# A depthwise convolution of 31 taps shared out anew between TensorE, VectorE and GpSimd

## The chip, the cores and the metric

The program runs on one core of one Trainium2 chip. A core has five engines that work side by side, each through its own queue in order: TensorE (PE; PEld is its weight load), VectorE (DVE), ScalarE (ACT), GpSimd (POOL) and SyncE (SP, which here only issues DMAs). The metric is the device time of one execution in microseconds; lower is better.

## The reference, cut to what matters

Two transformer blocks on 256 tokens with 1024 features: the first is SwiGLU, mixed attention, SwiGLU; the second is a convolution module, a feed-forward layer, an attention layer and another feed-forward layer. The change lies in the convolution module:

```python
def conformer_conv(hn, w_pw1, b_pw1, w_dw, b_dw, ln_g, ln_b, w_pw2, b_pw2):
    u = hn @ w_pw1 + b_pw1
    a, g = jnp.split(u, 2, axis=-1)
    u = a * jax.nn.sigmoid(g)
    u = lax.conv_general_dilated(u, w_dw[:, None, :], ...,       # depthwise: each channel by itself,
            padding=((30, 0),), feature_group_count=D_MODEL) + b_dw   # 31 taps back in time
    u = layernorm(u, ln_g, ln_b)
    u = jax.nn.silu(u)
    return u @ w_pw2 + b_pw2
```

## The kernel before

**Tiles.** Activations lie feature-major: 128 features on the partitions, 256 tokens along the free axis, so 1024 features are 8 tiles of 128x256.

**Weights.** All large weights come through one stream of chunks of 128x1024 (`in_wts`): SP loads a chunk into `raw` (5 buffers), ACT copies it to a rounded upper part `hi` (L231), and DVE subtracts to get the lower part `lo` (L235); `hi` and `lo` have 4 buffers each. A chunk holds 8 blocks of 128x128, and each block is used by three matmuls of 256 columns (L252 to L254: upper weights by upper activations, upper by lower, lower by upper), so 24 matmuls per chunk. In the stage "conv" a split is one instruction of 1024 columns; in other late stages it is two of 512.

**The convolution stage** (`conv`, L1126 to L1230) loops over 8 tiles. `pw1(n)` makes the two halves of tile n with 2 x 8 blocks (two chunks, so 16 chunks for the stage), DVE scales both out of PSUM (L1153, L1156), ACT applies tanh and bias, DVE joins them into `cu`, 30 columns of zeros and then 256 tokens (L1160). The zeros are GpSimd memsets (L1159). ACT also copies the tile into `cx`, with even and odd tokens on two halves of the partitions (L1166); its 32 columns of zeros are GpSimd memsets too (L1163), and `cx` has two buffers.

`conv_out(n)` shares the 31 taps. With `LAGS = 11`, TensorE does the last 21 taps as 11 matmuls in plain float32 for each half of the tile (L1181), with the taps on diagonals of 128x128 matrices `cw`, loaded by SP (9 of 16), or `dw`, built on DVE during the SwiGLU before (7 of 16, `tap_matrices`). ACT puts the result back in place as `cb` (L1184). `REST = TAPS + 1 - 2 * LAGS` = 10 taps are left to DVE: two chains of multiply-adds over shifted views of `cu` (L1193 for the first of each chain, L1195 for the others), whose sums are added (L1196), and from tile 1 on shifted by the first tile's mean (L1198). `stats(n)` adds the two results (L1203) and adds to the sum and the sum of squares of the layer norm (L1217 and L368).

**What sets the order.** A scheduler with a timeline of its own lays out each engine's queue at build time; on the chip each engine then follows its queue in order, waiting on semaphores. The layer norm's sums (L376 on PE, bank `pt`) need all eight tiles; behind them the order is written by hand.

Of the kernel before, what the change touches and what calls it, by code (L numbers as in the profile page):

```python
# [9 lines left out]
F32 = mybir.dt.float32  # L10
# [3 lines left out]
ALU = mybir.AluOpType  # L14
AX = mybir.AxisListType

P = 128
T = 256
D = 1024
KD = D // P  # L20
# [7 lines left out]
TAPS = 31  # L28
LAGS = 11
# [87 lines left out]
class Kern:  # L117
# [28 lines left out]
    def phase(self, name):  # L146
        """A pool for the tiles of one phase; closed when the next one opens."""
        if self.ph is not None:
            self.ph.close()
        if name == "ffn0":  # L150
            self.taps.close()
        self.ph = ExitStack()
        self.cycle = CYCLE.get(name, CYCLE["ffn"])
        self.stage = name
        self.name = name
        self.pp = self.ph.enter_context(self.tc.tile_pool(name=name, bufs=2, reuse_waits="pool"))
        if name == "f2w2":
            self.taps = ExitStack()
            self.tp = self.taps.enter_context(self.tc.tile_pool(name="taps", bufs=1, side="right"))
# [25 lines left out]
    # weights  # L185
# [17 lines left out]
    def raw_chunk(self):  # L203
        """A chunk of weights as they are; raw_weight() says which."""
        self.loaded += 1
        raw = self.rawp.tile([P, CH * P], F32, tag="raw", name=self.nm("raw"))
        self.nc.sync.dma_start(raw, self.ap["wts"][self.loaded])
        return self.loaded, raw
# [5 lines left out]
    def prefetch(self, two=False):  # L214
        """Load and split one more chunk of the weights; or leave the lower parts to a second step."""
        nc = self.nc
        self.loaded += 1
        chunk = self.loaded
        raw = self.rawp.tile([P, CH * P], F32, tag="raw", name=self.nm("raw"))
        pieces = 2 if chunk == 0 else 1  # L220
        step = CH * P // pieces
        for i in range(pieces):
            s = slice(i * step, (i + 1) * step)
            nc.sync.dma_start(raw[:, s], self.ap["wts"][chunk, :, s])
        hi = self.hip.tile([P, CH * P], F32R, tag="hi", name=self.nm("hi"))
        lo = self.lop.tile([P, CH * P], F32R, tag="lo", name=self.nm("lo"))
        piece = PIECE.get(self.stage, 4)
        h = piece * P
        def high(i):
            s = slice(i * h, (i + 1) * h)  # L230
            nc.scalar.activation(hi[:, s], raw[:, s], AF.Copy)  # L231

        def low(i):
            s = slice(i * h, (i + 1) * h)
            nc.vector.tensor_tensor(lo[:, s], raw[:, s], hi[:, s].bitcast(F32), op=ALU.subtract)  # L235

        self.ready.append((chunk, hi, lo))
        n = CH // piece
        if two:
            for i in range(n):  # L240
                high(i)
            return lambda: [low(i) for i in range(n)]
        for i in range(n):
            high(i)
            low(i)

    def mm3(self, out, pairs, first=True, last=True):
        """out += sum over (stationary (hi, lo), moving (hi, lo)) pairs."""
        nc = self.nc
        n = len(pairs)  # L250
        for i, ((sh, sl), (mh, ml)) in enumerate(pairs):
            nc.tensor.matmul(out, sh, mh, start=(first and i == 0), stop=False)  # L252
            nc.tensor.matmul(out, sh, ml, start=False, stop=False)  # L253
            nc.tensor.matmul(out, sl, mh, start=False, stop=(last and i == n - 1))  # L254

    def dense(self, name, c0, X, width=P):
        """A feature-major output tile [width, T] in a bank."""
        b = self.bank()
        out = b[:width, :T]
        self.mm3(out, [(self.weight(name, k, c0, width), X[k]) for k in range(len(X))])  # L260
        return out

    def dense_steps(self, name, c0, X, done):
        """As dense(), in steps; done() takes the output."""
# [7 lines left out]
    def early_steps(self, name, n, X, outs):  # L272
        """The output tile n of a dense, from inputs that are still to come."""
# [7 lines left out]
    def fill(self, n):  # L281
        """n steps of the dense work in line."""
# [9 lines left out]
    def finish(self, key):  # L292
        """All steps in line up to those of a key."""
# [12 lines left out]
    def pipeline(self, units, start, second, lag, w, keep):  # L306
        """The units' stages, one unit behind the other, and the work in line between them,
        of which some is kept for the last units."""
# [24 lines left out]
    # splits  # L333
# [21 lines left out]
    # norms  # L355

    def square_into(self, acc, x, last=False):
        """x * x added to the sums acc; the last one stays a sum of its own."""
# [4 lines left out]
        else:  # L363
# [4 lines left out]
            nc.vector.tensor_tensor(acc[0], acc[0], sq, op=ALU.add)  # L368
        return acc

    def col_sums(self, parts, tag="pt", b=None):
        """[P, T] feature-major tiles -> [token, 2] sums over all features, in PSUM."""
# [9 lines left out]
    def rsqrt(self, v, n):  # L382
        """v [P, n] in SBUF, positive -> v ** -0.5."""
# [9 lines left out]
    def broadcast(self, rcol, copy=True):  # L393
        """[token, 2] -> [P, T] with the tokens along the free axis."""
# [16 lines left out]
    # blocks  # L411

    def setup(self):
# [25 lines left out]
        # the PE's clock rises while the first loads are under way  # L439
# [11 lines left out]
    def feed(self, x, gains, acc, last):  # L451
        """Split x * gain for each of the gain columns and add to the sum of squares."""
# [3 lines left out]
    def tap_matrices(self):  # L456
        """The steps that build the last depthwise matrices: taps on the diagonals of blocks."""
# [54 lines left out]
    def normed(self, gains):  # L512
        """An `after` that feeds the next norm, and what it collects."""
# [9 lines left out]
    def mix(self, X, rc, R, after):  # L523
# [5 lines left out]
        # rope tables with the key side's norm and the scale folded in  # L529
# [18 lines left out]
        def KV():  # L548
            # selected and window keys, both groups on both halves of the partitions
# [13 lines left out]
            # values and gates, token-major  # L563
# [18 lines left out]
        # compressed keys and values  # L582
# [18 lines left out]
        def compress_in(kv):  # L601
            """A block's 32 tokens, two to a column: [(token parity, d), token pair, (group, block)]."""
# [16 lines left out]
        def hidden(r):  # L619
            """Two of the 16 token pairs, on four column groups: (keys or values, half of the outputs)."""  # L620
# [52 lines left out]
        # queries of the second branch  # L673
# [46 lines left out]
        # compressed branch: probabilities of a group's heads, gated  # L720
# [45 lines left out]
        # selected and window branches  # L766
        Y = []

        def nsa_scores(h):
            """The probabilities of both branches, gated."""  # L770
# [30 lines left out]
        def nsa_unit(h):  # L801
            """Scores and probabilities; transposes; a pair's outputs."""
# [24 lines left out]
        # differential attention  # L827
# [34 lines left out]
        def v_at(dest, t, c0, w):  # L862
            """Columns c0.. of token tile t of a token-major value store."""
# [9 lines left out]
        def da_unit(h):  # L873
# [3 lines left out]
            # the second set's weights relative to the first's, which scales the sum at the end  # L877
# [55 lines left out]
        # what has to be in place a unit before it is used  # L933
# [70 lines left out]
    def v_steps(self, name, X, half, bks):  # L1004
        """Token-major outputs, 512 columns of both token tiles."""
# [13 lines left out]
    def bc(self, v, axis, n):  # L1019
        """v [P, m] broadcast to [P, n, m] (axis 1) or [P, m, n] (axis 2)."""  # L1020
# [4 lines left out]
    def softmax(self, parts, rcol):  # L1025
        """Causal exponentials of one score set, [128 q, (q1, k0) | (q1, k1) | (q0, k0)], and the
        reciprocals of their sums, [128 q, (q1, q0)]."""
# [33 lines left out]
    def transposed3(self, A):  # L1061
        """Blocks (q1, k0), (q1, k1), (q0, k0) -> [128 k, k0: q0 q1 | k1: q1]."""
# [11 lines left out]
    def residual(self, o, n, after):  # L1074
        """x[n] += o and the next norm's feed."""
# [50 lines left out]
    def conv(self, X, R, after):  # L1126
# [20 lines left out]
        def pw1(n):  # L1147
# [13 lines left out]
            # the two halves of the channels, even and odd tokens on the partitions  # L1161
# [9 lines left out]
        def conv_out(n, u, x):  # L1171
# [15 lines left out]
            # the other taps, in two chains; weights are halved and the sums with them  # L1187
# [8 lines left out]
            nc.vector.tensor_tensor(v[0], v[0], v[1], op=ALU.add)  # L1196
            if n:
                nc.vector.tensor_tensor(v[0], v[0], self.shift, op=ALU.add)  # L1198
            return v[0], back

        def stats(n, v, back):
            nonlocal acc, acc2
            nc.vector.tensor_tensor(v, v, back, op=ALU.add)  # L1203
            if n == 0:
                # all tiles are taken relative to the mean of the first one
# [9 lines left out]
            else:  # L1215
                if n < KD - 1:
                    nc.vector.tensor_tensor(acc, acc, v, op=ALU.add)  # L1217
            acc2 = self.square_into(acc2, v, n == KD - 1)
# [100 lines left out]
        # the first outputs side by side, as their inputs come  # L1319
# [9 lines left out]
    def fox(self, Xk, rc, R, after):  # L1329
# [11 lines left out]
        # the gates' sums in parts, for matmuls over four rows: rows 32 b + (0..3), column block s: head 4 b + s  # L1341
# [8 lines left out]
        def log_gates():  # L1350
            """Token-major: log sigmoid."""
# [20 lines left out]
        def gate_sums():  # L1372
            """Running sums over the tokens: hi, lo, -hi, -lo."""
# [55 lines left out]
        def head(h):  # L1429
            """Scores and probabilities; transposes; a pair's outputs."""  # L1430
# [79 lines left out]
    def run(self, out):  # L1510
# [23 lines left out]
        # the first block's last norm and the second's first, together  # L1534
# [59 lines left out]
def phased(w):  # L1594
    """[TAPS, D] -> the last 2 LAGS - 1 taps by even and odd tokens,
    [(tile, half), (parity in, channel), lag, parity out]:
    a channel's output 2 q + r takes its input 2 (q - lag) + p with tap 30 - (2 lag + r - p)."""
# [11 lines left out]
def blocks_of(d):  # L1609
    """Those taps on the diagonals of [64, 64] blocks."""  # L1610
# [6 lines left out]
def lay_out(inputs):  # L1617
    """The inputs other than the weights as the program reads them, and the weights by name."""
# [98 lines left out]
```

## Time and profile before

| | us |
|---|---|
| median of 3 runs (1405.17 to 1406.17) | 1406.08 |
| span of the profiled execution | 1404.9 |
| PE busy in it | 1387.4 (99%) |
| DVE busy | 1031.3 (73%) |
| ACT busy | 825.7 (59%) |
| POOL busy | 23.1 (2%) |

The span runs from the first instruction to the last of one execution; the median is 1.2 us above it. A busy share is the mean over all stages. What a change in one stage is worth is read in that stage, between about 700 and 794 us from the span's start here.

### The profile page before, as it was taken

What the parts mean: (1) busy time and instruction counts of PE and PEld (TensorE: products, weight loads), DVE (VectorE), ACT (ScalarE), POOL (GpSimd) and SP (SyncE); (2) the same over time, 40 slices, a digit from 0 to 9 for tenths busy, and PEclk for the clock granted to TensorE, in tenths of its full rate; (3) what the DMA queues carried; (4) which work ended last, traced back from release to release, by engine and by line L of the source; (5) the groups of instructions that cost most, each with busy time, mean ns of one, the idle gap of its engine ahead of it and who ended that gap; (6) DMA issues with size and microseconds to landing.
All of it is one profiled execution on the core that took longest, in us unless ns stands there. A gap on an engine that the chain in (4) does not pass through costs nothing.

```text
span 1404.9 us, 28855 instructions
## 1 busy us (share of the span) xinstructions
PE 1387.4 (99%) x11223; PEld 1341.1 (95%) x11223; DVE 1031.3 (73%) x2295; ACT 825.7 (59%) x1869; POOL 23.1 (2%) x54
## 2 busy tenths in 40 slices
PE   9999999999999999999999999999999999999997
PEld 8999998999989999999999999999988889999997
DVE  7777659788877778876689887655597766775555
ACT  6555445677787455545555686654476665665444
POOL 0000000000000000000000000000000000000000
PEclk9999999999999999999999999999999999999998
DMA  7555557543333555655574156555555324655551
GB/s 270 182 187 187 181 177 256 194 136 106 106 106 104 187 178 180 192 184 181 181 261 160 56 171 210 182 186 187 166 180 160 105 84 132 206 181 180 182 186 38
DMA packets 65466, 234.94 MB, mean 167 GB/s; under 512 B 7569, under 2 KB 8305, under 8 KB 65329
## 3 DMA queue, kind: packets, MB, share of 16 engines
q1 hardware_dynamic: 63792, 231.42, 50.3%
q8 instruction: 88, 1.44, 0.4%
q10 hardware_dynamic: 1376, 1.42, 0.3%
q0 software_dynamic: 160, 0.26, 0.1%
q14 instruction: 50, 0.40, 0.1%
HBM read 231.95 MB, written 1.05 MB: 166 GB/s over the span
## 4 chain that ended last, share of the span: by engine, by line
PE 95%; DVE 2%; DMA 1%; ACT 1%; issue 0%; POOL 0%; POOLq 0%; DVEq 0%; SPq 0%; ACTq 0%
PE mm L252 12%; PE mm L253 12%; PE mm L254 12%; PE at L252 8%; PE at L253 8%; PE at L254 8%; PE s L252 7%; PE s L254 7%; PE s L253 7%; PE s L1033 3%; PE pt L1181 3%; PE pt L1066 1%; PE at L819 1%; DVE lo L235 1%; PE mm L1015 1%; PE mm L1013 1%
## 5 line engine op out<-in xcount | busy, mean ns | idle before, releaser
L231 ACT ACTIVATE hi<-raw 128x512 fp32r<-128x512 f32 (+1 forms) x760 | 474.0, 666 | 434.5 <-issue 249.0
L235 DVE TENSOR_TENSOR lo<-raw,hi 128x512 fp32r<-128x512 f32 (+1 forms) x760 | 536.4, 740 | 168.8 <-ACT hi L231 166.2
L252 PE MATMUL mm<-a,hi 128*128 128x256 f32 x1046 | 305.1, 292 | 1.0 <-ACT hi L231 1.0
L253 PE MATMUL mm<-a,hi 128*128 128x256 f32 x1046 | 296.7, 284 | 0.0
L254 PE MATMUL mm<-a,lo 128*128 128x256 f32 x1046 | 296.3, 283 | 0.0
L252 PEld LDWEIGHTS mm<-a,hi 128*128 128x128 f32 x1046 | 200.7, 192 | 3.7 <-issue 2.3
L253 PEld LDWEIGHTS mm<-a,hi 128*128 128x128 f32 x1046 | 200.6, 192 | 0.0
L254 PEld LDWEIGHTS mm<-a,lo 128*128 128x128 f32 x1046 | 200.2, 191 | 0.2 <-DVE lo L235 0.2
L252 PE MATMUL at<-a,hi 128*128 128x256 f32 x622 | 177.7, 286 | 2.0 <-ACT hi L231 2.0
L254 PE MATMUL at<-a,lo 128*128 128x256 f32 x622 | 177.6, 286 | 0.2 <-DVE lo L235 0.2
L253 PE MATMUL at<-a,hi 128*128 128x256 f32 x622 | 177.6, 286 | 0.0
L252 PE MATMUL s<-a,hi 128*128 128x256 f32 x516 | 147.2, 285 | 1.0 <-ACT a L1263 1.0
L254 PE MATMUL s<-a,lo 128*128 128x256 f32 x516 | 146.9, 285 | 0.2 <-DVE lo L235 0.2
L253 PE MATMUL s<-a,hi 128*128 128x256 f32 x516 | 146.8, 285 | 0.0
L252 PEld LDWEIGHTS at<-a,hi 128*128 128x128 f32 x622 | 119.1, 192 | 2.8 <-ACT hi L231 2.2
L254 PEld LDWEIGHTS at<-a,lo 128*128 128x128 f32 x622 | 119.5, 192 | 1.3 <-DVE lo L235 0.4
L253 PEld LDWEIGHTS at<-a,hi 128*128 128x128 f32 x622 | 119.2, 192 | 0.7 <-DVE a L346 0.5
L252 PEld LDWEIGHTS s<-a,hi 128*128 128x128 f32 x516 | 99.5, 193 | 1.3 <-ACT a L1263 1.2
L254 PEld LDWEIGHTS s<-a,lo 128*128 128x128 f32 x516 | 99.5, 193 | 0.4 <-DVE lo L235 0.4
L253 PEld LDWEIGHTS s<-a,hi 128*128 128x128 f32 x516 | 99.5, 193 | 0.0
L253 PE MATMUL at<-H,hi 128*128 128x256 f32 x324 | 91.9, 284 | 0.0
L254 PE MATMUL at<-H,lo 128*128 128x256 f32 x324 | 91.8, 283 | 0.0
(408 smaller groups left out, 2816.0 us busy)
## 6 DMA issues: line engine op xcount, KB each, us to landing
raw<-in_wts SPq DMA_DIRECT2D x424, 512.0 KB, 3.5
cw<-in_dwp SPq DMA_DIRECT2D x9, 704.0 KB, 4.0
x<-in_xT SPq DMA_DIRECT2D x4, 256.0 KB, 5.8
raw<-in_wts SPq DMA_DIRECT2D x2, 256.0 KB, 5.3
e<-in_pT ACTq DMA_DIRECT2D x4, 128.0 KB, 4.4
out_dram<-o ACTq DMA_DIRECT2D x2, 256.0 KB, 3.0
out_dram<-o SPq DMA_DIRECT2D x2, 256.0 KB, 2.8
cst<-in_cst SPq DMA_DIRECT2D x1, 416.0 KB
```

The lines of the kernel that those rows point to most:

```text
L231: nc.scalar.activation(hi[:, s], raw[:, s], AF.Copy)
L235: nc.vector.tensor_tensor(lo[:, s], raw[:, s], hi[:, s].bitcast(F32), op=ALU.subtract)
L252: nc.tensor.matmul(out, sh, mh, start=(first and i == 0), stop=False)
L253: nc.tensor.matmul(out, sh, ml, start=False, stop=False)
L254: nc.tensor.matmul(out, sl, mh, start=False, stop=(last and i == n - 1))
L819: nc.tensor.matmul(o[e * HD : (e + 1) * HD, kt * P :], V[:, kt, 2 * i + g], pt[i][:, k], start=False, stop=(i == 1 and kt == 1),)
L1013: nc.tensor.matmul(bks[t], xh, wk[0], start=(k == 0), stop=False)
L1015: nc.tensor.matmul(bks[t], xh, wk[1], start=False, stop=(k == KD - 1))
L1033: nc.tensor.matmul(o, q[:, t * P : n], k[:, :n], start=(t == 1 and i == 0), stop=False)
L1066: nc.tensor.transpose(tb[:, o * P : (o + 1) * P], a, self.ident)
L1181: nc.tensor.matmul(o, w[:, d], x[:, g, 16 - d : 16 + P - d], start=(d == 0), stop=(d == LAGS - 1))
```

## The change

Two numbers move the share of the taps, and three kinds of elementwise work go from VectorE to GpSimd:

- `LAGS` 11 to 8: TensorE keeps 15 taps (8 matmuls for each half of a tile), and `REST` goes from 10 to 16 taps on VectorE. The matrices `cw` and `dw` shrink from 11 to 8 blocks.
- In the stage "conv", GpSimd makes `lo` of the weights.
- GpSimd makes four additions for a tile: the two chains' sum, the shift, the sum and the sum of squares.

```diff
-LAGS = 11
+LAGS = 8
...
         def low(i):
             s = slice(i * h, (i + 1) * h)
-            nc.vector.tensor_tensor(lo[:, s], raw[:, s], hi[:, s].bitcast(F32), op=ALU.subtract)
+            e = nc.gpsimd if self.stage == "conv" else nc.vector
+            e.tensor_tensor(lo[:, s], raw[:, s], hi[:, s].bitcast(F32), op=ALU.subtract)
...
-    def square_into(self, acc, x, last=False):
+    def square_into(self, acc, x, last=False, engine=None):
...
-            nc.vector.tensor_tensor(acc[0], acc[0], sq, op=ALU.add)
+            (engine or nc.vector).tensor_tensor(acc[0], acc[0], sq, op=ALU.add)
...
-            nc.vector.tensor_tensor(v[0], v[0], v[1], op=ALU.add)
+            nc.gpsimd.tensor_tensor(v[0], v[0], v[1], op=ALU.add)
             if n:
-                nc.vector.tensor_tensor(v[0], v[0], self.shift, op=ALU.add)
+                nc.gpsimd.tensor_tensor(v[0], v[0], self.shift, op=ALU.add)
...
                 if n < KD - 1:
-                    nc.vector.tensor_tensor(acc, acc, v, op=ALU.add)
-            acc2 = self.square_into(acc2, v, n == KD - 1)
+                    nc.gpsimd.tensor_tensor(acc, acc, v, op=ALU.add)
+            acc2 = self.square_into(acc2, v, n == KD - 1, nc.gpsimd)
```

The rest of the diff takes out comments; from L235 on the lines of the changed kernel stand one higher. In the rows below a name's number is that of its buffer.

GpSimd's queue from the two reciprocal roots on (`rs_y`) that open the stage. Before:

```order
L385 TENSOR_TENSOR rs_y_9655<-rs_v_9653,mhalf 128x2
L385 TENSOR_TENSOR rs_y_9663<-rs_v_9661,mhalf 128x2
L1163 MEMSET cx_9980 128x2x16
L1159 MEMSET cu_10239 128x30
L1163 MEMSET cx_10114 128x2x16
L1159 MEMSET cu_10367 128x30
```

After:

```order
L386 TENSOR_TENSOR rs_y_9655<-rs_v_9653,mhalf 128x2
L386 TENSOR_TENSOR rs_y_9663<-rs_v_9661,mhalf 128x2
L236 TENSOR_TENSOR lo_9914<-raw_9911,hi_9913 128x1024
L236 TENSOR_TENSOR lo_9944<-raw_9941,hi_9943 128x1024
L236 TENSOR_TENSOR lo_10048<-raw_10045,hi_10047 128x1024
L236 TENSOR_TENSOR lo_10078<-raw_10075,hi_10077 128x1024
L236 TENSOR_TENSOR lo_10176<-raw_10173,hi_10175 128x1024
L236 TENSOR_TENSOR lo_10206<-raw_10203,hi_10205 128x1024
L236 TENSOR_TENSOR lo_10304<-raw_10301,hi_10303 128x1024
L1164 MEMSET cx_9980 128x2x16
L1197 TENSOR_TENSOR a_9890<-a_9890,t_9891 128x256
L1160 MEMSET cu_10239 128x30
```

Seven of the twelve splits that are left at this point stand in a row, with tile 0's sum of chains (`a_9890`) behind them; the other four splits of the stage stand ahead of the roots.

VectorE's queue where tile 0 is finished (`a_9896` before, `a_9890` after). Before:

```order
L1195 SCALAR_TENSOR_TENSOR t_9897<-cu_9778,dww_9703,t_9897 128x256
L1195 SCALAR_TENSOR_TENSOR t_10030<-cu_9855,dww_9703,t_10030 128x256
L1160 SCALAR_TENSOR_TENSOR cu_10111<-u_10105,th_10108 128x256
L1195 SCALAR_TENSOR_TENSOR t_10158<-cu_9977,dww_9703,t_10158 128x256
L1196 TENSOR_TENSOR a_9896<-a_9896,t_9897 128x256
L1156 TENSOR_TENSOR th_10236<-at_10171,R_9674 128x256
L1193 TENSOR_SCALAR t_10286<-cu_10111,dww_9703 128x256
L1195 SCALAR_TENSOR_TENSOR t_10158<-cu_9977,dww_9703,t_10158 128x256
L1203 TENSOR_TENSOR a_9896<-a_9896,cb_9865 128x256
L235 TENSOR_TENSOR lo_10430<-raw_10427,hi_10429 128x1024
```

After:

```order
L1196 SCALAR_TENSOR_TENSOR t_9891<-cu_9778,dww_9703,t_9891 128x256
L1196 SCALAR_TENSOR_TENSOR t_10152<-cu_9977,dww_9703,t_10152 128x256
L1154 TENSOR_TENSOR u_10105<-mm_10044,R_9674 128x256
L1196 SCALAR_TENSOR_TENSOR t_10024<-cu_9855,dww_9703,t_10024 128x256
L1196 SCALAR_TENSOR_TENSOR t_10152<-cu_9977,dww_9703,t_10152 128x256
L1204 TENSOR_TENSOR a_9890<-a_9890,cb_9865 128x256
L1196 SCALAR_TENSOR_TENSOR t_10024<-cu_9855,dww_9703,t_10024 128x256
```

The sum of the chains and the split have left VectorE's queue, and its next step on tile 0 (L1204, was L1203) now waits for GpSimd; taps of other tiles stand behind it.

The stage's end. On VectorE before:

```order
L1195 SCALAR_TENSOR_TENSOR t_10702<-cu_10617,dww_9703,t_10702 128x256
L1196 TENSOR_TENSOR a_10701<-a_10701,t_10702 128x256
L1198 TENSOR_TENSOR a_10701<-a_10701,cm_9989 128x256
L1203 TENSOR_TENSOR a_10659<-a_10659,cb_10632 128x256
L1217 TENSOR_TENSOR acc_9993<-acc_9993,a_10659 128x256
L368 TENSOR_TENSOR acc_9995<-acc_9995,sq_10717 128x256
L1203 TENSOR_TENSOR a_10701<-a_10701,cb_10674 128x256
```

On GpSimd after:

```order
L1197 TENSOR_TENSOR a_10653<-a_10653,t_10654 128x256
L1199 TENSOR_TENSOR a_10653<-a_10653,cm_9989 128x256
L1197 TENSOR_TENSOR a_10695<-a_10695,t_10696 128x256
L1218 TENSOR_TENSOR acc_9993<-acc_9993,a_10653 128x256
L1199 TENSOR_TENSOR a_10695<-a_10695,cm_9989 128x256
L369 TENSOR_TENSOR acc_9995<-acc_9995,sq_10717 128x256
```

The last tile's sum, its shift and the running sums have moved to GpSimd's queue; VectorE keeps only the two additions of `cb` there.

## Rows read from the trace of the kernel before

**Rows 1.** The page, busy time by engine and granted TensorE clock in 40 slices

```profile
PE   9999999999999999999999999999999999999997
PEclk9999999999999999999999999999999999999998
```

**Rows 2.** Stretches: length, then busy us (instructions) of PE, PEld, DVE, ACT, POOL, clock

```profile
716.00:760.00 44.00, 44.00 (x379) 43.95 (x378) 43.92 (x106) 25.99 (x55) 0.87 (x7) 1.00 0.66 226
760.00:793.60 33.60, 33.05 (x291) 32.86 (x289) 26.83 (x66) 21.24 (x55) 0.37 (x3) 1.00 0.21 69
```

**Rows 3.** Chain that ended last, 786 to 800 us: start, us, what

```profile
789.45 2.45 PE pt L1181 x22
...
793.58 1.68 PE pt L376 x16
```

**Rows 4.** Stretch 716 to 793.6, L1181 alone: length, PE busy (records), PEld busy

```profile
716.00:793.60 77.60, 41.32 (x352) 40.38 (x352) 1.00 0.46 158
```

**Rows 5.** DVE's groups, 715 to 800: line, tiles, shapes, count | busy us, mean ns

```profile
L1195 DVE SCALAR_TENSOR_TENSOR t<-cu,dww,t 128x256 f32<-128x256 f32 x32 | 14.9, 480 | 0.0
```

**Rows 6.** DVE's timeline: start, us from first start to last end, what

```profile
709.77 0.20 DVE L1139 TENSOR_SCALAR dww<-dww 128x80 f32<-128x80 f32 x1 [2.86 <-DMA dww<-in_dww]
...
713.62 2.35 DVE L235 TENSOR_TENSOR lo<-raw,hi 128x1024 fp32r<-128x1024 f32 x2
...
716.56 0.41 DVE L1153 TENSOR_TENSOR u<-mm,R 128x256 f32<-128x256 f32 x1
...
717.55 2.77 DVE L1548 TENSOR_TENSOR a<-a,R 128x256 f32<-128x256 f32 x8
...
742.52 1.14 DVE L1193 TENSOR_SCALAR a<-cu,dww 128x256 f32<-128x256 f32 x4
...
747.88 1.67 DVE L1195 SCALAR_TENSOR_TENSOR a<-cu,dww,a 128x256 f32<-128x256 f32 x4
...
760.67 1.28 DVE L235 TENSOR_TENSOR lo<-raw,hi 128x512 fp32r<-128x512 f32 x2
```

**Rows 7.** The end of the stage on PE and DVE, timeline

```profile
787.53 0.48 DVE L1195 SCALAR_TENSOR_TENSOR t<-cu,dww,t 128x256 f32<-128x256 f32 x1
...
793.41 0.28 PE L376 MATMUL pt<-ones,acc 128*128 128x1 f32 x2
```

**Rows 8.** DVE building the `dw` matrices: ns min/median/max, first and last start

```profile
L472 DVE TENSOR_TENSOR dw<-dmask,dwt x7: 1618/1619/1621, 535.6 to 571.3; 128x1408 f32<-128x1408 f32 x7
```

**Rows 9.** POOL: the longest memset (timeline) and the short ones (group)

```profile
1044.60 1.81 POOL L1343 MEMSET C<- 128x2048 f32 x1 [28.13 <-DVE a L1077]
...
L1163 POOL MEMSET cx<- 128x32 f32 x6 | 0.7, 124 | 60.3 <-PE pt L1181 57.9 <-ACT sq L365 2.4
```

**Rows 10.** DVE beside that memset, timeline

```profile
1044.64 1.85 DVE L1339 TENSOR_SCALAR tri<-maskb 128x128 f32<-128x128 bf16 x1
1046.52 0.29 DVE L1340 TENSOR_TENSOR tri<-tri,cst 128x128 f32<-128x128 f32 x1
```

**Rows 11.** A root on POOL beside two-input work on DVE, timelines

```profile
1049.03 1.40 POOL L385 TENSOR_TENSOR rs_y<-rs_v,mhalf 128x2 f32<-128x2 f32 x1 [2.62 <-DVE rs_v L390]
...
1048.80 0.47 DVE L346 SCALAR_TENSOR_TENSOR a<-a,cols,a 128x256 fp32r<-128x256 f32 x1
1049.19 0.68 DVE L235 TENSOR_TENSOR lo<-raw,hi 128x512 fp32r<-128x512 f32 x1
1049.79 0.48 DVE L346 SCALAR_TENSOR_TENSOR a<-a,cols,a 128x256 fp32r<-128x256 f32 x1
```

**Rows 12.** Splits on DVE that begin under POOL work: a root, a memset

```profile
344.34 0.69 POOL L385 TENSOR_TENSOR rs_y<-rs_v,mhalf 128x2 f32<-128x2 f32 x1 [5.34 <-DVE rs_v L390]
...
344.56 1.23 DVE L235 TENSOR_TENSOR lo<-raw,hi 128x1024 fp32r<-128x1024 f32 x1 [0.36 <-ACT hi L231]
...
203.36 0.53 POOL L593 MEMSET vc<- 128x512 f32 x1
...
203.22 1.23 DVE L235 TENSOR_TENSOR lo<-raw,hi 128x1024 fp32r<-128x1024 f32 x1
```

## The prediction

> **What bounds the kernel now.** I read first the page's busy shares and slices: TensorE is busy at 99%, in every slice but the last, at a granted clock of 1.0, the 2.4 GHz level [rows 1]. So an edit gains only if it takes work off TensorE, or a wait that TensorE feels, and it loses as soon as another engine makes TensorE wait. Then I read the convolution stage by stretches [rows 2]. From 716 to 760 us both PE (44.00 of 44.00) and DVE (43.92) are full; from 760 to 793.6 PE is full (33.05 of 33.60) and DVE has 6.8 us free. The chain of waits runs on PE through L1181 and leaves the stage at the layer norm's sums, L376 [rows 3]; the first of them starts at 793.41 [rows 7]. GpSimd does 1.24 us of work in these 77.6 us [rows 2]. Third, the timeline of DVE: its records overlap, so I take the distance from start to start, not the duration. Four multiply-adds of 256 columns span 1.67 us with 0.48 for the last [rows 5, 6], so one takes (1.67 - 0.48) / 3 = 0.396 us. In the same way an addition of two tiles takes (2.77 - 0.41) / 7, rounded 0.335 us, with 0.41 for one; a first tap at most 1.14 / 4 = 0.285; a split of 1024 columns 2.35 - 1.23 = 1.12, and a split in two halves about 1.2, 1.28 less the overlap [rows 6, 12].
>
> **What leaves TensorE.** 16 half tiles lose 3 matmuls each. L1181 has 352 records for 16 x 11 = 176 matmuls [rows 4], so a float32 matmul is two records, and 22 of them take 2.45 us [rows 3]: 0.111 us a record. 16 x 3 x 2 = 96 records are 10.7 us. All of it lies on the chain. TensorE alone would reach the sums at 793.4 - 10.7 = 782.7 us.
>
> **What VectorE gets and gives.** It gets 6 x 8 = 48 multiply-adds, 48 x 0.396 = 19.0 us. It gives 16 splits, 16 x 1.12 = 17.9 us, of which four lie ahead of the stage, and 8 + 7 + 6 + 6 = 27 additions, 27 x 0.335 = 9.0 us. The matrices `dw` are built from 1024 columns instead of 1408, 7 x about 0.4 us less [rows 8], in a stage where PE is full and DVE is not; I cost that, and the smaller loads of `cw`, at nothing.
>
> The stage's new length on DVE, from its first scaling at 716.56 [rows 6]: 14 x 8 = 112 multiply-adds 44.4 us, 16 first taps 4.6, 16 scalings out of PSUM 5.4, and 8 + 8 + 6 additions of the kinds L1160, L1548 and L1203 7.4; the first tile's shift 0.9, four half-by-half splits for the layer norm 4.8, two small ones 0.7. That is 68.2 us and ends the last tap at 784.8. Behind it the order has three additions on GpSimd (0.5 to 0.7 each, below), one on DVE (0.41), a square on ACT (about the same) and the sums: about 3.3 us, so 788.1. Before, the last tap began at 787.53 and the sums at 793.41 [rows 7]. **Without any new wait the stage ends 5.3 us sooner**, bound by DVE and not by TensorE (782.7).
>
> The opening of the stage I cost at nothing. On DVE the taps' table (709.77, after 2.86 us of waiting for its DMA [rows 6]) now stands ahead of the first root's input, so the root is paid behind it, about 1 us; against that three splits (3.4 us) leave DVE's queue ahead of `R`. If both misfire this is 2 us.
>
> **What GpSimd gets.** 16 splits of 1024 and 27 additions of 256 columns, all with two inputs and one output in SBUF. The trace has no such instruction of any length on GpSimd. A memset of 2048 columns takes 1.81 us and one of 32 0.124 [rows 9]: 0.84 ns a column for one pass. At the low end reading costs nothing more (one pass); at the high end two reads and a write come one after another (three passes, 2.52 ns) and each instruction also pays the 0.69 us that a root of two columns takes [rows 12]. I take the middle between two and three passes, 2.1 ns: a split 2.15 us, an addition 0.54. GpSimd's work is then 16 x 2.15 + 27 x 0.54 = 49 us, less than the 68 of DVE. The Trainium skill ("GPSIMD Engine Reference", §3.1) gives 4497 ns for an addition of 2048 columns, 2.2 ns a column, and advises against elementwise work there; no run here shows that figure yet. By it the sum below would come out 1.4 us higher.
>
> **What decides is whether GpSimd and VectorE can work at the same time.** Two rows say that they can block each other for whole instructions. A `tensor_scalar` of 128 columns that began 0.04 us after the memset of 1.81 us took 1.85 us, and its neighbour of the same size 0.29 [rows 10]: it was held until the memset's end. And a root on GpSimd took 1.40 us where it takes 0.69 elsewhere; it was issued at 1049.03 while DVE was in a multiply-add, and DVE's next instruction, a split, began at 1049.19 ahead of it [rows 11]. The extra 0.71 us is the rest of the multiply-add and that split. Two other rows speak less clearly: a split that began 0.22 us into a root ran at its usual 1.23, and so did one that began under a memset [rows 12]. A root has two columns to read, which is over at once, and a memset reads nothing. So what collides is reading two inputs on both engines, which is what all the moved work does, and what 134 of DVE's instructions in the stage do.
>
> The Trainium skill ("SBUF — State Buffer", section "Who interferes with whom") states it so: a VectorE instruction with two SBUF inputs contends with a GpSimd instruction that reads SBUF, and who comes second waits for the whole of the other; it speaks against this change. Rows 11 and 12 agree with it for short instructions; that long ones hold each other for their whole length no row here shows.
>
> **The forecast** follows these rows: reading instructions of the two engines run one after another. Of the 16 splits four stand ahead of the roots in GpSimd's queue and are done before the stage, and about two more before 716.5; of the additions the last three stand behind the last tap. So 10 x 2.15 + 24 x 0.54 = 34.5 us of GpSimd lie between 716.5 and the last tap. GpSimd can hide under DVE's scalings out of PSUM, of which I count half, 2.7 us. DVE's last tap moves by 31.8 us, and the stage ends 31.8 - 5.3 = 26.5 us later. TensorE then waits, since its 77.05 - 10.7 = 66 us of work [rows 2] are spread over 104. The chain would carry DVE's taps and GpSimd's splits in turn. Behind the sums nothing changes. Against the profiled span that is 1404.9 + 26.5 = 1431.4, and the median lies 1.2 us above the span: **1432.6 us**. With one pass (0.86 and 0.215 us) the held time is 13.8 and the result +5.8, 1411.9; with two passes +19.5, with three +33.3, 1439.4; with three passes and 0.69 us an instruction +56.6, 1462.7.
>
> **Rivals.** *No holding.* GpSimd reads beside DVE at no cost. Then the stage ends 5.3 us sooner: 1400.8, **faster**, and DVE is the bound. It can lose some of it: GpSimd's queue has tile 0's sum behind seven splits and ahead of five, and VectorE's L1204 waits for it. Seven splits from about 712 end at 727 at the earliest, and tile 0's 16 taps at about 733 (43 instructions of DVE's queue), so DVE is not held there. For it: the normal splits under a root and a memset [rows 12]. Against it: the root of 1.40 us [rows 11]. It decides only if long reads pass each other. 1398 to 1404.
>
> *Sharing by columns.* The two engines use one path in turn, column by column, not instruction by instruction. DVE needs it for the columns only: (1.12 - 0.335) / 768 = 1.02 ns a column, 0.26 us of the 0.396. 134 x 0.26 + 4.2 for the columns of four splits + 4.6 for first taps = 43.6 us, and GpSimd's 34.5 fill the rest: 78.1 us instead of 68.2, so 9.9 - 5.3 = +4.6: 1410.7; where GpSimd needs the path only in part, down to 1400. For it: nothing here excludes it for long instructions. Against it: the `tensor_scalar` that was held to the memset's end [rows 10].
>
> *Starved splits.* DVE goes ahead whenever both wait, as the split at 1049.19 did [rows 11]. Then `lo` comes late, PE stands still, DVE runs out of inputs, and only then GpSimd works. The sum of the two engines is the same; what is added is the wait of PE's queue for a last chunk, 24 matmuls at 44.00 / 379 = 0.116 us [rows 2], 2.8 us, and the chain of the last tile. This is the forecast's upper side, up to some 1448.
>
> **How the numbers follow.** Holding, with starving as its upper part: 0.66. Sharing: 0.17, of which 0.04 is faster, 0.06 the same and 0.07 slower. No holding: 0.17, of which 0.15 is faster by over 0.2% (2.8 us, about what a measurement of this kernel can tell from no change) and 0.02 is not. So faster 0.19, same 0.08, slower 0.73. The holding case alone reaches from 1412 to 1463; I leave out what needs 0.69 us on top of three passes, and below it keep the sharing case and half of the other: 1400 to 1448.
>
> **What would show it.** In the profile after: L1182 with 256 records, 10.7 us less, in any case. If I am right, multiply-adds on DVE of 0.8 to 2.5 us among those of 0.48, ending where a GpSimd instruction ends; GpSimd's splits longer than in a quiet place; PE with gaps from about 725 on, waiting for `lo` from GpSimd or for `cb` and `cu`; the first L377 at about 820. If DVE's multiply-adds keep 0.48 us, no holding is right, and that L377 comes near 788. A mean a little above 0.48 for all of them, with no long ones, is sharing. I would be wrong in size if a split on GpSimd takes well under 1.7 us or over 2.6, and wrong in place if PE waits first for something that the opening delays, `R` above all.

## The result

| | before | changed |
|---|---|---|
| median, us | 1406.12 (4 runs, 1405.17 to 1409.17) | 1438.71 (4 runs, 1437.74 to 1440.74) |
| span of the profiled execution, us | 1404.9 | 1437.6 |

The changed kernel is slower: ratio 1.0224, with a 95% interval of 1.0209 to 1.0240, which is 32.6 us. The spans differ by 32.7 us. The forecast was 1432.6 in a range of 1400 to 1448.

### The profile page after: what moved, and what is told of

Its sections match the earlier page's. It is cut to its first block, busy times and chain, and to the rows that moved or that the text cites. A ratio compares the mean times of both kernels' runs of the same rounds, so it can differ in the third digit from the quotient of the medians.

```text
span 1437.6 us, 28721 instructions
## 1 busy us (share of the span) xinstructions
PE 1387.2 (96%) x11127; PEld 1339.0 (93%) x11127; DVE 1062.0 (74%) x2300; ACT 824.3 (57%) x1869; POOL 88.4 (6%) x97
## 3 DMA queue, kind: packets, MB, share of 16 engines
q10 hardware_dynamic: 1376, 1.42, 0.3%
## 4 chain that ended last, share of the span: by engine, by line
PE 87%; DVE 9%; DMA 1%; ACT 1%; POOL 1%; issue 1%; POOLq 0%; DVEq 0%; SPq 0%; ACTq 0%
PE mm L253 12%; PE mm L254 11%; PE mm L255 11%; PE at L254 7%; PE at L255 7%; PE at L253 7%; PE s L253 6%; PE s L255 6%; PE s L254 6%; PE s L1034 3%; DVE t L1196 2%; DVE a L1196 2%; PE pt L1067 1%; PE at L820 1%; DVE lo L236 1%
## 5 line engine op out<-in xcount | busy, mean ns | idle before, releaser
L236 DVE TENSOR_TENSOR lo<-raw,hi 128x512 fp32r<-128x512 f32 (+1 forms) x744 | 517.4, 730 | 163.0 <-ACT hi L231 160.5
L253 PE MATMUL at<-H,hi 128*128 128x256 f32 x324 | 91.7, 283 | 0.0
L254 PE MATMUL at<-H,hi 128*128 128x256 f32 x324 | 91.7, 283 | 0.0
```

What stands on the lines that cost most here:

```text
L236: e.tensor_tensor(lo[:, s], raw[:, s], hi[:, s].bitcast(F32), op=ALU.subtract)
```

## The profile after

The lines of the changed kernel's code stand one below those of before (L1196 was L1195, L1182 was L1181, L377 was L376). The page of the changed kernel first: busy time by engine, the rows of the 40 slices that answer to [rows 1], with VectorE's and GpSimd's beside them, and the shares of the chain by engine.

```profile
PE 1387.2 (96%) x11127; PEld 1339.0 (93%) x11127; DVE 1062.0 (74%) x2300; ACT 824.3 (57%) x1869; POOL 88.4 (6%) x97
...
PE   9999999999999999999868699999999999999997
...
DVE  7776668788876778766699888765578776776555
...
POOL 0000000000000000000453500000000000000000
PEclk9999999999999999999989899999999999999999
...
PE 87%; DVE 9%; DMA 1%; ACT 1%; POOL 1%; issue 1%; POOLq 0%; DVEq 0%; SPq 0%; ACTq 0%
```

PE has a hole at slices 20 to 23, where GpSimd works: the convolution stage, and nowhere else. The stretches of [rows 2] and the one that the stage now also fills, in the same columns (length, busy us and instructions of PE, PEld, DVE, ACT, POOL, granted clock, DMA share, GB/s):

```profile
716.00:760.00 44.00, 30.40 (x215) 29.78 (x216) 43.00 (x72) 16.14 (x34) 22.86 (x12) 0.81 0.44 132
760.00:793.60 33.60, 29.00 (x237) 28.80 (x237) 33.60 (x61) 16.13 (x35) 17.10 (x19) 0.96 0.41 126
793.60:826.00 32.40, 19.52 (x141) 18.41 (x140) 27.46 (x58) 15.62 (x42) 16.44 (x19) 0.87 0.16 49
826.00:868.00 42.00, 40.88 (x319) 40.67 (x319) 33.96 (x84) 31.05 (x71) 0.70 (x1) 0.93 0.39 126
```

From 716 to 760 VectorE is as busy as before (43.00 us of 44.00), but with 72 instructions in the place of 106. PE ran 215 records where it ran 379. An engine that is full and does less has longer instructions. VectorE's groups between 724.6 and 820.7 us (line, tiles, shapes, count | busy us, mean ns | idle us before) say which, and one group that keeps its length:

```profile
L1196 DVE SCALAR_TENSOR_TENSOR t<-cu,dww,t 128x256 f32<-128x256 f32 x56 | 34.3, 630 | 0.0
L1196 DVE SCALAR_TENSOR_TENSOR a<-cu,dww,a 128x256 f32<-128x256 f32 x56 | 32.3, 596 | 0.0
L236 DVE TENSOR_TENSOR lo<-raw,hi 128x512 fp32r<-128x512 f32 x8 | 6.3, 811 | 0.0
L1161 DVE SCALAR_TENSOR_TENSOR cu<-u,th 128x256 f32<-128x256 f32 x8 | 6.3, 783 | 0.0
L1194 DVE TENSOR_SCALAR a<-cu,dww 128x256 f32<-128x256 f32 x8 | 5.1, 657 | 0.0
L1204 DVE TENSOR_TENSOR a<-a,cb 128x256 f32<-128x256 f32 x6 | 4.8, 804 | 1.4 <-POOL a L1199 1.4
L1194 DVE TENSOR_SCALAR t<-cu,dww 128x256 f32<-128x256 f32 x8 | 4.8, 600 | 0.0
...
L1154 DVE TENSOR_TENSOR u<-s,R 128x256 f32<-128x256 f32 x3 | 1.2, 414 | 0.0
```

The multiply-adds, 480 ns before [rows 5], have means of 630 and 596. The mean hides two kinds. The summary of that line's records (count: ns min/median/max, first and last start) has about the median of before (472 ns; 480 there) and a maximum more than five times as long:

```profile
L1196 DVE SCALAR_TENSOR_TENSOR a<-cu,dww,a x56: 468/472/2623, 733.8 to 819.8; 128x256 f32<-128x256 f32 x56
```

One of the long ones in the timelines of GpSimd and of VectorE (start, us, instruction, idle time before in brackets):

```profile
761.53 2.48 POOL L236 TENSOR_TENSOR lo<-raw,hi 128x1024 fp32r<-128x1024 f32 x1 [7.29 <-ACT hi L231]
...
761.72 2.57 DVE L1196 SCALAR_TENSOR_TENSOR t<-cu,dww,t 128x256 f32<-128x256 f32 x1
```

The split ends at 764.01, the multiply-add at 764.29: it was held until the split was over and then did its 0.3 us. A scaling out of PSUM during a GpSimd addition keeps its usual time:

```profile
779.31 0.93 POOL L1197 TENSOR_TENSOR a<-a,t 128x256 f32<-128x256 f32 x1 [2.73 <-DVE a L1196]
...
779.55 0.41 DVE L1154 TENSOR_TENSOR u<-at,R 128x256 f32<-128x256 f32 x1
```

The chain that ended last, pieces between 690 and 835 us (start, us, what), answers to [rows 3]:

```profile
694.26 2.52 DVE a L509
...
717.88 4.65 DVE diag L400 x2
...
771.42 2.49 DVE a L1196
...
823.05 0.72 POOL acc L1218
...
825.47 3.14 PE pt L377 x14
```

In the place of PE's L1181 it runs through VectorE's held instructions, and through GpSimd's sums at the end. The last sums begin at 825.47, where [rows 3] had 793.58.

The stage begins late as well. GpSimd's and VectorE's timelines at its opening:

```profile
714.83 0.70 POOL L386 TENSOR_TENSOR rs_y<-rs_v,mhalf 128x2 f32<-128x2 f32 x1 [1.37 <-DVE rs_v L391]
715.49 6.95 POOL L236 TENSOR_TENSOR lo<-raw,hi 128x1024 fp32r<-128x1024 f32 x3
...
715.56 2.28 DVE L1544 TENSOR_TENSOR rr<-r,rs_y 128x2 f32<-128x2 f32 x1 [0.87 <-POOL rs_y L386]
717.88 4.63 DVE L400 TENSOR_SCALAR diag<-cst,rr 128x128 f32<-128x128 f32 x2
722.44 0.47 DVE L400 TENSOR_SCALAR diag<-cst,r 128x128 f32<-128x128 f32 x2
...
724.60 0.42 DVE L1154 TENSOR_TENSOR u<-mm,R 128x256 f32<-128x256 f32 x1
```

Right behind the second root three splits run on GpSimd, and VectorE's next three instructions take one split each: a product of two columns (2.28 us), and two diagonals (4.63). A pair of diagonals without a split beside it takes 0.47. They stand ahead of `R`. The four splits ahead of the roots do the same to four instructions of the norm before: the one at 694.26 in the chain above and three more take 2.42 to 2.72 us, where instructions of their lines take 0.42 to 0.48 in the kernel before, and the chain runs through three of the four. The first scaling comes at 724.60 where it came at 716.56 [rows 6].

## The experiments

Three theories were set against each other. **Holding** is the forecast's: instructions that read two inputs from SBUF on GpSimd and on VectorE run one after another. **Late GpSimd**: nothing is held, GpSimd is merely slow, and those who need `lo` and the sums wait for it. **Overloaded VectorE**: the 48 new multiply-adds alone cost the time. Edits are given against the changed kernel, but for the last, which is given against the kernel before. The kernel before had medians of 1406.60 and 1407.09 beside these runs.

**The taps alone.** GpSimd gets nothing.

```diff
-            e = nc.gpsimd if self.stage == "conv" else nc.vector
+            e = nc.vector
...
-            nc.gpsimd.tensor_tensor(v[0], v[0], v[1], op=ALU.add)
+            nc.vector.tensor_tensor(v[0], v[0], v[1], op=ALU.add)
```

(and so the other three additions)

> Only the share of the taps is changed (LAGS 8); GpSimd gets no splits and no additions. Holding (reading instructions of GpSimd and VectorE run one after another): VectorE's own work in the stage is 68.2 us as reckoned before, plus 12 splits x 1.12 and 27 additions x 0.335, 90.7 us, nothing is held and the opening is as in the kernel before, so the sums come near 809 instead of 793.4 and the time is about 1421 us (1416 to 1426), some 18 us below the changed kernel. Late GpSimd (GpSimd's work is simply slow and what needs it comes late; nothing is held): also about 1421. Overloaded VectorE (16 taps a tile are too many, whatever GpSimd does): as the changed kernel, 1435 to 1442.

Measured: 1421.45 (1420.47 to 1422.37), ratio 1.0106 [1.0089, 1.0123]. First scaling at 715.81, last tap at 800.19. The multiply-adds take 476 to 486 ns, none is held. So the taps cost 15 us, somewhat less than half of the loss: VectorE becomes the bound (busy for all of the 33.60 us from 760 to 793.6), and *Overloaded VectorE* explains that part only.

**GpSimd's work alone.**

```diff
-LAGS = 8
+LAGS = 11
```

> Only GpSimd's part of the change: splits and additions on GpSimd, 11 lags on TensorE and 10 taps on VectorE as before. Holding: VectorE's own work is 68.2 - 19.0 = 49.2 us, held for some 28 us as in the changed kernel, behind an opening that is 8 us late; TensorE's 77 us of work start from that late opening too, so the sums come at 802 to 808 and the time is about 1418 us (1413 to 1424). Overloaded VectorE: its work falls by 19 + 9 + 13 us against the kernel with 16 taps and all on VectorE, so 1406 or a little less. Late GpSimd: 1410 to 1420.

Measured: 1426.14 (1423.92 to 1426.62), ratio 1.0139 [1.0124, 1.0154]: 2 us above the range of the holding theory, and 6 above that of *Late GpSimd*. The first scaling is at 724.35, late by the same opening. The longest multiply-add is 2628 ns, in VectorE's records of L1196:

```profile
L1196 DVE SCALAR_TENSOR_TENSOR t<-cu,dww,t x32: 471/476/2628, 734.1 to 807.0; 128x256 f32<-128x256 f32 x32
```

With VectorE's old number of taps, relieving it of splits and additions costs 20 us.

**One of GpSimd's two tasks at a time**: the splits alone, then the additions alone (the edits above, one half each).

> The changed kernel with its 27 additions back on VectorE; GpSimd keeps the 16 splits. Holding: VectorE gets 27 x 0.335 = 9.0 us of work, and the additions' holds (about 7 us) and the tail's hand-overs through GpSimd (about 3 us) go; 1437 us (1432 to 1442), near the changed kernel: additions of either engine cost VectorE about the same. Overloaded VectorE: 9 us more, about 1448. Late GpSimd: GpSimd has a third less to do, so clearly less, 1420 to 1430.

Measured: 1434.98 (1434.55 to 1438.80), ratio 1.0207 [1.0190, 1.0223].

> The changed kernel with its 16 splits back on VectorE; GpSimd keeps the 27 additions. Holding: VectorE gets 12 x 1.12 = 13.4 us in the stage and loses about 21 us of holds, and the opening is as early as before (8 us), so about 1423 us (1417 to 1428). Overloaded VectorE: 13 us more than the changed kernel, about 1450. Late GpSimd: about 1420.

Measured: 1425.78 (1422.92 to 1427.33), ratio 1.0133 [1.0116, 1.0150]. VectorE's records of L1196 in the first and in the second of them:

```profile
L1196 DVE SCALAR_TENSOR_TENSOR t<-cu,dww,t x56: 471/478/2599, 736.6 to 818.4; 128x256 f32<-128x256 f32 x56
```

```profile
L1196 DVE SCALAR_TENSOR_TENSOR t<-cu,dww,t x56: 472/481/949, 728.7 to 808.7; 128x256 f32<-128x256 f32 x56
```

Both times lie in the ranges of *Holding* and outside of the other two, the additions' only 6 us from *Late GpSimd*. The length of a hold follows what GpSimd runs: up to 2.6 us beside splits of 2.4, up to 0.95 beside additions of 0.72. Over the taps alone the splits add 13.5 us and the additions 4.3. Their sum, 17.8, is near to what both add in the changed kernel, 1438.71 - 1421.45 = 17.3. So each of the two moves loses by itself.

**The same occupancy without the reading.** This is the test between *Holding* and *Late GpSimd*: each split is a subtraction of two columns and three memsets, so that GpSimd is as long occupied and `lo` is as late. It leaves out the lower parts of that stage's weights.

```diff
-            e.tensor_tensor(lo[:, s], raw[:, s], hi[:, s].bitcast(F32), op=ALU.subtract)
+            e.tensor_tensor(lo[:, :w] if w == 2 else lo[:, s], ...)
+            if w == 2:
+                for r in (1024, 1024, 512):
+                    nc.gpsimd.memset(lo[:, :r].bitcast(F32), 0.0)
```

> The changed kernel with each of GpSimd's 16 splits replaced by a subtraction of 2 columns and three memsets of 1024, 1024 and 512 columns over the same tile: GpSimd is as long busy (about 2.4 us) at the same places of its queue, but reads almost nothing. The lower parts of that stage's weights are left out by this. Holding: multiply-adds on VectorE keep 0.48 us beside the memsets; left are the additions' holds (about 7 us) and short holds of first taps and of the two scaled identities in the opening, so the time is about 1414 us (1407 to 1421). Late GpSimd: GpSimd's occupation and its order are kept, so as the changed kernel, 1433 to 1441.

Measured: 1417.22 (1416.82 to 1418.71), ratio 1.0080 [1.0065, 1.0095]. That is 21.5 us less than the changed kernel. GpSimd's largest group between 690 and 825 us, and the records of VectorE's multiply-adds (L1201 here):

```profile
L241 POOL MEMSET lo<- 128x1024 f32 x32 | 30.4, 953 | 1.0
```

```profile
L1201 DVE SCALAR_TENSOR_TENSOR t<-cu,dww,t x56: 467/474/1001, 721.9 to 799.5; 128x256 f32<-128x256 f32 x56
```

With the shorter memsets (8.5 us) and the subtractions (5.1) GpSimd is occupied for 44.0 us, and the splits of the changed kernel took 39.4. The holds of 2.6 us are gone; the longest multiply-add, 1.0 us, stands beside the additions that are left. The first scaling is back at 715.35. *Late GpSimd* forecast the changed kernel's time here, and falls for the splits.

Then the additions, meant in the same way: two columns and a memset of 640 columns of a spare tile. This one leaves out the sums of 254 columns as well.

```diff
+    def two(self, out, a, b):
+        self.nc.gpsimd.tensor_tensor(out[:, :2], a[:, :2], b[:, :2], op=ALU.add)
+        self.nc.gpsimd.memset(self.junk, 0.0)
...
-            nc.gpsimd.tensor_tensor(v[0], v[0], v[1], op=ALU.add)
+            self.two(v[0], v[0], v[1])
```

> As the run with write-only splits, and GpSimd's additions too are 2 columns and a memset of 640 columns of a spare tile: nothing of length that reads is left on GpSimd. Left out are the lower parts of that stage's weights and 254 of 256 columns of the moved additions. Holding: VectorE runs its 68.2 us almost without holds (first taps, 2 to 5 us), so about 1406 us (1400 to 1412), near the 1400.8 that was reckoned for no holding. Late GpSimd: 1428 to 1440.

Measured: 1405.46 (10 runs, 1403.42 to 1407.05), ratio 0.9993 [0.9984, 1.0002]. The memsets of the spare tile did not run where they were meant to. All 27 ran within the first 23 us of the execution (L367 here), far ahead of the stage, so the additions are merely short in this run, and their occupancy is not kept:

```profile
L367 POOL MEMSET junk<- x27: 631/632/802, 0.7 to 22.1; 128x640 f32 x27
```

GpSimd's groups between 690 and 825 us:

```profile
L241 POOL MEMSET lo<- 128x1024 f32 x32 | 30.3, 951 | 1.0
L241 POOL MEMSET lo<- 128x512 f32 x16 | 8.6, 536 | 0.5
```

The records of VectorE's multiply-adds (L1207 here):

```profile
L1207 DVE SCALAR_TENSOR_TENSOR a<-cu,dww,a x56: 464/474/481, 724.6 to 790.6; 128x256 f32<-128x256 f32 x56
```

VectorE's groups between 718.4 and 791.5 us, its first taps:

```profile
L1205 DVE TENSOR_SCALAR a<-cu,dww 128x256 f32<-128x256 f32 x8 | 5.0, 646 | 0.0
L1205 DVE TENSOR_SCALAR t<-cu,dww 128x256 f32<-128x256 f32 x8 | 4.1, 516 | 0.0
```

GpSimd is occupied for 30.3 + 8.6 us by the memsets that replace the splits (39.4 us by the splits themselves in the changed kernel), and no multiply-add is held: 464 to 481 ns. The last sums begin at 792.50. So 21.5 us hang on the splits' reading alone, by the run before this one. The other 11.8 (1417.22 - 1405.46) are what the additions cost by their reading and their length together. That additions hold is shown by the records of up to 0.95 us above; how much of the 11.8 is holding was not tested.

Even this kernel gains nothing that can be told from zero. By the profiled executions, its stage takes 74.1 us from the first scaling to the last sums, and that of the kernel before 77.0. What it gains there it loses behind the sums, where the granted clock is 0.52 from 792.50 to 799.10 us (the last section has more on this). VectorE's first taps are still held, since a memset holds a `tensor_scalar`, as in [rows 10]: 646 and 516 ns, where the taps alone have 349 and 350.

**The opening.** The first seven splits stay on VectorE.

```diff
-            e = nc.gpsimd if self.stage == "conv" else nc.vector
+            if self.stage == "conv":
+                self.nsplit = getattr(self, "nsplit", 0) + 1
+            e = nc.gpsimd if self.stage == "conv" and self.nsplit > 7 else nc.vector
```

> The changed kernel with the stage's first seven splits, those that run before and at the broadcast R, back on VectorE; nine stay on GpSimd. Holding: the 8 us by which R is late go, three splits of 1.12 stand on VectorE for as many holds of 2.1 less; 1429 us (1425 to 1433). Late GpSimd without holding: R does not depend on it, so 1436 to 1440.

Measured: 1431.10 (1430.04 to 1433.16), ratio 1.0178 [1.0161, 1.0195]. VectorE's timeline at the opening:

```profile
711.01 0.16 DVE L1546 TENSOR_TENSOR rr<-r,rs_y 128x2 f32<-128x2 f32 x1 [0.87 <-POOL rs_y L388]
...
712.26 0.48 DVE L402 TENSOR_SCALAR diag<-cst,rr 128x128 f32<-128x128 f32 x2
...
715.98 0.42 DVE L1156 TENSOR_TENSOR u<-mm,R 128x256 f32<-128x256 f32 x1
```

The two-column product takes 0.16 us again (2.28 in the changed kernel) and the pair of diagonals 0.48 (4.63). The first scaling comes 8.6 us sooner, the last tap 7.8, and the end 7.6. The opening's delay is real, is made by the early splits, and passes through to the end almost whole.

**Can the idea be had without GpSimd?** The kernel before with 10 lags (two more taps on VectorE) and the first taps on ScalarE:

```diff
-LAGS = 11
+LAGS = 10
...
-                    nc.vector.tensor_scalar(w, s, c, None, op0=ALU.mult)
+                    nc.scalar.mul(w, s, c)
```

> Not the changed kernel but the one before, with 10 lags instead of 11 (12 taps on VectorE) and the first tap of each of the two chains on ScalarE instead of VectorE; GpSimd gets nothing. TensorE loses 16 x 2 records of 0.111 us, 3.6 us; VectorE gets 16 multiply-adds of 0.396 and gives 16 first taps of up to 0.285, +1.8 us in a stage where it has 6.8 us free; ScalarE gets 16 x about 0.4. If VectorE's free time lies where it is needed, up to 3 us faster, 1403 us; if not, no change, 1406. Holding and late GpSimd both say nothing here; overloaded VectorE: slower by some us.

Measured: 1405.23 (12 runs, 1401.58 to 1409.41), ratio 0.9991 [0.9981, 1.0001]. The last tap starts at 787.48 and the last sums at 790.61. In this profile, of the fastest of the 12, the sums come 3 us sooner than in the kernel before, but the ratio can't be told from no change. No version was found that beats the kernel before.

## Why the prediction was right, and where its terms were off

The mechanism was the forecast's, and the sum came within 6.1 us, partly because errors of both signs met. By its own steps:

| step | forecast | measured |
|---|---|---|
| L1182's records | 256 | 256 (144 + 112) |
| VectorE's own work, first scaling to last tap, us | 68.2 | 68.6 (below) |
| opening, first scaling late by, us | 0, bound 2 | 8.0 |
| a split / an addition on GpSimd, us | 2.15 / 0.54 | 2.41 / 0.72 |
| held time in the stage, us | 31.8 | 27.8 |
| last tap to the last sums, us | 3.3 | 4.9 |
| the sums late by, us | 26.5 | 31.9 |
| the end late by, us | 26.5 | 32.7 |

**TensorE's relief and VectorE's own time** were right. The kernel whose GpSimd only writes has no held multiply-adds: from 718.43 to the end of the last tap at 791.44 is 73.0 us. Of that its first taps are held for 8 x (646 - 349) + 8 x (516 - 350) = 3.7 us, and VectorE is idle for 0.7. 73.0 - 4.4 = 68.6.

**The opening was the step that failed.** The prediction asked what of GpSimd's work lies before the stage, found about six splits there, and counted them as free. It should have asked what VectorE has in its queue beside them, and who waits for that. It even named `R` as the place where it would be wrong. Three splits behind the second root held three short instructions on which every scaling depends, 3 x 2.3 us less their own 0.6, 6.3 us. Another 4.0 came before them: the two-column product starts at 715.56, and in VectorE's timeline of the kernel before it starts at 711.58:

```profile
711.58 0.16 DVE L1543 TENSOR_TENSOR rr<-r,rs_y 128x2 f32<-128x2 f32 x1 [0.86 <-POOL rs_y L385]
```

The splits ahead of the roots held VectorE, the table of taps came at 711.95 and not at 709.77 [rows 6], and the first root's input stood behind it, for which the prediction had about 1 us. `R`'s two copies waited 0.9 us for TensorE, and the three splits that left VectorE's queue gave back their 3.4, as the prediction said: 6.3 + 4.0 + 0.9 - 3.4 = 7.8 of the 8.0. The rows for it were there: in [rows 10] a `tensor_scalar` of this kind was held for a memset's length, and the diagonals are `tensor_scalar`s.

**The held time** was over by 4.0 us, in two parts that offset each other. GpSimd's work was priced too low: from the first scaling to the last tap 9 splits and 22 additions, 9 x 2.41 + 22 x 0.72 = 37.5 us, and not 34.5. GpSimd's groups in the changed kernel (690 to 830 us) give means with the waits in them:

```profile
L236 POOL TENSOR_TENSOR lo<-raw,hi 128x1024 fp32r<-128x1024 f32 x16 | 39.4, 2472 | 197.6 <-ACT hi L231 195.3 <-PE pt L1182 2.4
L1197 POOL TENSOR_TENSOR a<-a,t 128x256 f32<-128x256 f32 x8 | 10.5, 1317 | 22.4 <-DVE t L1196 19.0 <-DVE a L1196 3.4
```

The records of the splits (ns min/median/max):

```profile
L236 POOL TENSOR_TENSOR lo<-raw,hi x16: 2342/2410/3002, 694.1 to 774.2; 128x1024 fp32r<-128x1024 f32 x16
```

The middle between two and three passes was too low, three (2.52 ns x 1024 = 2.58) a little too high. The Trainium skill ("GPSIMD Engine Reference", §3.1) gives 4497 ns for 2048 columns. By half of that a split would be an estimated 2.25 us, and the shortest here took 2.34.

And less of that work was felt. The lengthening of the seven groups shown above, count by mean less the time without a hold (472, 678, 418, 340 ns), is 8.8 + 6.9 + 1.1 + 2.9 + 2.5 + 2.3 + 2.1 = 26.6 us, and VectorE was idle for 1.8 more. So about 10 of the 37.5 us hid beside VectorE, and not 2.7: under scalings out of PSUM, in the first part of an instruction that is held only from then on, and in waits of GpSimd's own.

The Trainium skill's rule ("SBUF — State Buffer", sections "Who interferes with whom" and "Summary: rules for kernel authors"), that the second of two such instructions to issue waits until the first is finished, agrees with the splits here (the multiply-add of 761.72, above). It doesn't cover all that is here. The prediction counted [rows 12] as agreeing with it; the split there that began 0.22 us into a root and took its usual 1.23 shows no wait. And at the end of the stage VectorE went ahead (GpSimd's timeline, then VectorE's):

```profile
809.22 3.28 POOL L1197 TENSOR_TENSOR a<-a,t 128x256 f32<-128x256 f32 x1 [4.66 <-DVE t L1196]
...
813.83 0.90 POOL L1218 TENSOR_TENSOR acc<-acc,a 128x256 f32<-128x256 f32 x1 [0.54 <-DVE a L1204]
```

```profile
809.46 0.47 DVE L1196 SCALAR_TENSOR_TENSOR t<-cu,dww,t 128x256 f32<-128x256 f32 x1
...
811.44 0.47 DVE L1196 SCALAR_TENSOR_TENSOR a<-cu,dww,a 128x256 f32<-128x256 f32 x1
...
814.07 0.95 DVE L1196 SCALAR_TENSOR_TENSOR a<-cu,dww,a 128x256 f32<-128x256 f32 x1
```

The addition of 809.22 waited until VectorE had nothing ready, through six multiply-adds that began behind it at their usual 0.47 us. Another, at 819.12, took 2.09. At 813.83 the two took turns. What decides who goes first isn't settled by these runs. This is the rival *Starved splits* at two places, with additions and not splits, and it is small: VectorE's idle time behind the first of them is 1.42 us.

**The tail** was 4.9 us. The last addition on VectorE (L1204) is itself held, 0.93 us, and stands behind two additions of 0.72 on GpSimd.

**The sum** so corrected: 26.5 + 8.0 - 4.0 + 1.6 = 32.1 us, and the sums are 31.9 late.

**Behind the sums** the prediction said that nothing changes. The next norm's sums begin at 869.75, not 834.86, 34.9 late: 3 us more were lost between 826 and 868, where the granted clock is 0.93 (the last section has the cause). The span is 32.7 longer, so 2.2 us come back later. Nothing ties them to the change: from the reciprocal root at 1049.03 to the one at 1190.09 the profiled execution of the kernel before takes 141.1 us and that of the changed kernel 139.5, and of the eight other profiles seven have 139.5 and one 141.1, whatever their edit; between the last two roots it is 24.5 us or 23.9 in the same way.

**The other rivals.** *No holding* and *Sharing by columns* fall by the multiply-adds of 2.6 us beside a median of 472 ns: there are long ones, and the others are not lengthened.

## What to carry to other kernels

Price a move to GpSimd not by whether GpSimd has room, but by what VectorE runs meanwhile: two-input work out of SBUF on both engines runs mostly one after the other, and here taking 16 splits and 27 additions off VectorE, some 27 us of its time, made the kernel 17 us slower. Look at every place where the moved instructions may run, also ahead of the stage: a two-column product in a chain of short steps is held as long as a multiply-add. To test for it, keep the other engine as long occupied without reading; if the time comes back, it was the collision and not the lateness. Then look in the trace whether the stand-in work ran where it was meant to: here the memsets for the splits did, and those for the additions ran some 700 us early.

## What the runs showed that was not expected

- A product of two columns was held for 2.28 us, as long as any other. How much the held instruction reads made no difference. Nor were only instructions with two inputs held by splits: the diagonals and the first taps are `tensor_scalar`s of one tile.
- A memset on GpSimd leaves multiply-adds alone (464 to 481 ns) and holds `tensor_scalar`s (646 and 516 ns in the mean, 350 without). In one kernel both were seen.
- TensorE's granted clock fell where VectorE made it wait: 0.81 from 716 to 760 us, in which TensorE was busy for 30.40 of 44.00 us. The matmuls of that stretch show both levels, 2.4 GHz and 1.2: the longest record is twice the median.

```profile
L1182 PE MATMUL pt<-cx,cw x144: 270/275/582, 733.5 to 794.3; 128*128 128x128 f32 x144
```

In the stage VectorE was the bound. Behind it TensorE is (40.88 of 42.00 us busy from 826 to 868), and there the lower clock costs the 3 us: the granted clock is 0.51 from 825.47 to 832.00, and the sums take 3.14 us in the chain above where [rows 3] had 1.68. From the last sums to the next norm's root the kernel before takes 42.3 us and the changed one 45.3. In all ten profiles this stretch is 42.3 where the sums run at the higher level (the kernel before, GpSimd's work alone, ten lags) and 45.0 to 45.5 where they run at the lower one (the other seven). So a stage that lets TensorE wait is paid for a second time behind it.
